# Small tiles regrouped and padded so that every large SBUF tile begins on a multiple of 128 bytes

## The chip, the cores and the metric

The kernel runs on one core of a Trainium2 chip. Its time is the device time of one launch in microseconds (us); the number compared is the median over several runs. The engines are named as in the profile: PE (TensorE, matmuls; PEld is its weight load), DVE (VectorE), ACT (ScalarE), POOL (GpSimd) and SP (SyncE, which here only issues DMAs). SBUF is the on-chip memory of 128 partitions; an address in this text is a byte offset within a partition, the same in every partition.

## The reference

A two-layer decoder trunk over 512 tokens of width 1024, in float32. Each layer computes

```
x = x + 1/2 * swiglu(rmsnorm(x), ffn1)          # 1024 -> 2816 -> 1024
h = rmsnorm(x); p = h @ w_in                    # 1024 -> 6168 columns
x = x + concat(mlstm(p), ssd(p), convmodule(p)) @ w_out
x = x + 1/2 * swiglu(rmsnorm(x), ffn2)
```

and after both layers a last rmsnorm. `swiglu(h) = (silu(h @ wg) * (h @ wu)) @ wd`. mlstm and ssd are recurrences done in chunks of 128 tokens, the conv module is a depthwise convolution of width 31.

## The kernel before, in words

**Data and precision.** The residual x lies in SBUF transposed, as eight tiles xT[k] of 128 features by 512 tokens. A float32 product is made of three matmuls in a reduced type of 4 bytes: each operand is split into a high and a low part (xh/xl, whi/wlo, atile pairs, chi/clo), and high*high, high*low and low*high are accumulated in PSUM. Almost all of PE's work is such matmuls with a stationary operand of 128x128 (loaded by PEld) and a moving operand of 128x512 (2048 bytes in each partition).

**The families of matmuls.** They differ in which tile is stationary and which is moving:

- L189 to L191 (mm3) has a weight slice stationary (whi or wlo) and 512 tokens moving. In `contraction` the moving tile is an atile (the activations of a block), in `proj` it is xh or xl.
- L354 to L356 (product_halves in `gated`) has activations stationary and 512 weight columns moving (whi or wlo). The activations are slices of xh/xl, or of chi/clo, which hold sums and differences of x for a Strassen-like scheme: of the seven products of a block three take xh/xl and four take chi/clo.
- L877 to L879 (tok_proj, in the mixer) has xh/xl stationary and whi/wlo moving.
- L1059 to L1061 (Final.finish, the last contraction) has an atile stationary and whi/wlo moving: the form of L354 to L356 and L877 to L879, with other tiles.

```
189  nc.tensor.matmul(ps, wh, ah, start=start and k == 0, stop=False)     # out, stationary, moving
190  nc.tensor.matmul(ps, wh, al, start=False, stop=False)
191  nc.tensor.matmul(ps, wl, ah, start=False, stop=stop and k == n - 1)
354  nc.tensor.matmul(ps[t], ah, hv[:, i, :], start=start and k == 0, stop=False, **more)
355  nc.tensor.matmul(ps[t], ah, lv[:, i, :], start=False, stop=False, **more)
356  nc.tensor.matmul(ps[t], al, hv[:, i, :], start=False, stop=k == 3, **more)
877  nc.tensor.matmul(pv[c], xh[k][:, cs(c)], hv[:, k2, :], start=k == 0, stop=False)
1059 nc.tensor.matmul(ps, ah, hv[:, k - k0, :], start=k == 0, stop=False)
```

Every slice of these operands begins a multiple of 512 bytes past the start of its tile. Smaller matmuls in float32 proper (transposes such as L418, the scores and state products of the mixer such as L728, L807 and L839) make up the rest.

**The order of the work.** Each of the four FFNs is one first block of 256 hidden columns and five gated blocks of 512. A gated block is 168 matmuls of L354 to L356, 16 transposes (L418) and 96 matmuls of a contraction (L189 to L191). Between the two FFNs of a layer lies the mixer: projections (L189 to L191 with xh/xl moving, L877 to L879), the chunked recurrences, the 31-tap convolution as 30 DVE instructions per tile (L690), and contractions into xT. Weights stream from HBM into raw or half (SP queue), ACT casts them to whi (L175) and DVE makes wlo (L176), three buffers each. A scheduler orders the instructions by priority; addresses have no part in it.

**Where tiles lie.** A pool places its tiles one after the other in the order in which their tags are first asked for; each start is rounded up to 32 bytes, and a pool begins where the one before ends. The pools stand in the order const, wp, ap, tp, and then the phase's own pool (ff0, mix0, ff1, ...). const begins on a multiple of 128. Before the change:

| pool | tiles in order | start of the large tiles, modulo 128 |
|---|---|---|
| const (L93 to L108) | ident, ones, tri (512 bytes each), eps_r, eps_l (4 each, 32 taken), xT, xh, xl (24 of 2048), two upads, parameter columns | xT, xh, xl, upad: 64 |
| wp | raw (3 of 8192), whi and wlo (3 of 4096 each) | 0 |
| ap | 12 atiles of 2048 | 0 |
| tp | pst 512, ssq0 64 (L1125), ss, tmp (2048 each), rc 4 of 32, R 2048, nr 2 and den 4 of 32, fss 32 (L1052) | ss, tmp, R: 64 |
| FFN phases | half and chi/clo (4096 each), u (2048) | all: 32 |
| mixer phases | brow 224, dt to ecs 256 each, av, en, ws, dec, gw, arow, lt, rt, cacc, mtile, mc, rb, sc, small, wide, xb | cacc, mtile: 32; rb, sc, wide, first xb: 96 |

Of the kernel before, what the change touches and what calls it, by code (L numbers as in the profile page):

```python
# [20 lines left out]
F32 = mybir.dt.float32  # L21
# [6 lines left out]
P = 128  # L28
# [3 lines left out]
NCH = S // P  # L32
MH = 4
# [3 lines left out]
RMS_EPS = 1e-6  # L37
LN_EPS = 1e-5
# [11 lines left out]
def trunk(ctx: ExitStack, tc: tile.TileContext, I: dict, out: bass.AP):  # L50
    nc = tc.nc
# [4 lines left out]
    const = ctx.enter_context(tc.tile_pool(name="const", bufs=1))  # L56
    wp = ctx.enter_context(tc.tile_pool(name="wp", bufs=1))
    ap_ = ctx.enter_context(tc.tile_pool(name="ap", bufs=1))
    tp = ctx.enter_context(tc.tile_pool(name="tp", bufs=1))
# [12 lines left out]
    mp_ = Phase()  # L72
# [4 lines left out]
    def pacc():  # L77
        return ps_p.tile([P, S], F32, tag="acc", name="pacc")
# [4 lines left out]
    def tmp():  # L83
        return tp.tile([P, S], F32, tag="t", name="tmp", bufs=6)
# [4 lines left out]
    def mtile():  # L89
        return mp_.tile([P, S], F32, tag="m", name="mtile", bufs=9)  # L90


    ident = const.tile([P, P], F32, name="ident")  # L93
    make_identity(nc, ident)
    ones = const.tile([P, P], F32, name="ones")
# [1 line left out]
    tri = const.tile([P, P], F32, name="tri")  # L97
    nc.gpsimd.affine_select(tri, ones, pattern=[[1, P]], base=0, channel_multiplier=-1,
                            compare_op=ALU.is_ge, fill=0.0)
    eps_r = const.tile([P, 1], F32, name="eps_r")  # L100
    nc.vector.memset(eps_r, RMS_EPS)
    eps_l = const.tile([P, 1], F32, name="eps_l")
    nc.vector.memset(eps_l, LN_EPS)

    xT = [const.tile([P, S], F32, name=f"xT{k}") for k in range(KT)]
    xh = [const.tile([P, S], F32R, name=f"xh{k}") for k in range(KT)]
# [1 line left out]
    upads = [const.tile([P, S + CK - 1], F32, name=f"upad{i}") for i in range(2)]  # L108
    for t in upads:
        nc.gpsimd.memset(t[:, 0:CK - 1], 0.0)  # L110

    @contextmanager
    def shifted(n):
# [30 lines left out]
    def stream(src, nk, n):  # L144
        with shifted(-early[0]):
            raw = wp.tile([P, 2048], F32, tag="raw", name="raw", bufs=3)
            v = raw[:, :nk * n].rearrange("p (k n) -> p k n", n=n)
            k0 = c0 = 0
            for s in src if isinstance(src, list) else [src]:
                k, w = s.shape[1:]  # L150
                nc.sync.dma_start(v[:, k0:k0 + k, c0:c0 + w], s)
                k0, c0 = (k0, c0 + w) if k == nk else (k0 + k, c0)
        return v
# [14 lines left out]
    def split_w(v):  # L168
        with shifted(-early[0]):
            nk, n = v.shape[1], v.shape[2]  # L170
            hi = wp.tile([P, 1024], F32R, tag="whi", name="whi", bufs=3)
            lo = wp.tile([P, 1024], F32R, tag="wlo", name="wlo", bufs=3)
            hv = hi[:, :nk * n].rearrange("p (k n) -> p k n", n=n)
            lv = lo[:, :nk * n].rearrange("p (k n) -> p k n", n=n)
            nc.scalar.copy(hv, v)  # L175
            nc.vector.tensor_tensor(lv, v, hv.bitcast(F32), op=sub)  # L176
        return hv, lv
# [44 lines left out]
    class Norm:  # L222
# [24 lines left out]
        def finish(self):  # L247
            self.R = tp.tile([P, S], F32, tag="R", name="R", bufs=1)
            with shifted(AFTER):
                self.r = tp.tile([P, NCH], F32, tag="nr", name="nr", bufs=2)  # L250
                stat(self.ss, D, eps_r, self.r) if self.sums is None else rstd_cols(self.sums, D, eps_r, self.r)
                nc.scalar.copy(self.R, rows(self.r))
            return self
# [237 lines left out]
    def mixer(l, nrm, par, nxt):  # L491
# [4 lines left out]
        def cols(c0, n):  # L496
            return W[:, :, c0:c0 + n]
# [3 lines left out]
        nc.gpsimd.dma_start(graw[:, :, 0:8], cols(C_I, 8))  # L501
        nc.gpsimd.dma_start(graw[:, :, 8:24], cols(C_DT, 16))
        brow = mp_.tile([P, 56], F32, tag="brow", name="brow")
        nc.gpsimd.dma_start(brow[:, 0:8], I["mlstm_gate_b"][l:l + 1, :].partition_broadcast(P))
        nc.gpsimd.dma_start(brow[:, 8:24], I["ssd_dt_bias"][l:l + 1, :].partition_broadcast(P))
        nc.gpsimd.dma_start(brow[:, 24:40], I["ssd_a_log"][l:l + 1, :].partition_broadcast(P))
# [2 lines left out]
        sm = lambda n, nm: mp_.tile([P, n], F32, tag=nm, name=nm)  # L509
# [6 lines left out]
        av = sm(16, "av").rearrange("p (c h) -> p c h", h=MH)  # L516
        en = sm(16, "en").rearrange("p (c h) -> p c h", h=MH)
        ws = sm(12, "ws").rearrange("p (c h) -> p c h", h=MH)
        dec = sm(8, "dec")
        ml_rows = dr.tile([MH, 7 * P], F32, tag="ml_rows", name="ml_rows", bufs=1)  # L520
        ml_dec = dr.tile([1, MH * 2], F32, tag="ml_dec", name="ml_dec", bufs=1)
        cs = lambda c: slice(c * P, (c + 1) * P)
# [2 lines left out]
        def gates():  # L525
# [15 lines left out]
            part = lambda o, n: scratch[:, o:o + n]  # L541
# [8 lines left out]
            s1 = part(176, 80).rearrange("p (c h) -> p c h", h=20)  # L550
            s2 = part(256, 80).rearrange("p (c h) -> p c h", h=20)
            lp = part(336, 80).rearrange("p (c h) -> p c h", h=20)
            arow = sm(16, "arow")
            with tc.issue_after(nc.scalar.activation(e, gt[:, :, 4:24], AF.Abs).ins):
                nc.scalar.activation(arow, brow[:, 24:40], AF.Exp)
            nc.scalar.activation(e, e, AF.Exp, scale=-1.0)
# [47 lines left out]
                nc.tensor.transpose(pl[0:MH, c * P:(c + 1) * P], lc[:, c, 0:4], ident)  # L604
            nc.vector.tensor_copy(ar, pa[0:MH, :])
            nc.vector.tensor_copy(lr, pl[0:MH, :])
            mc = sm(16, "mc")[0:MH, :]
            for c in range(NCH):
                init = NEG if c == 0 else mc[:, c - 1:c]
                nc.vector.tensor_tensor_scan(Mx[:, cs(c)], ar[:, cs(c)], ar[:, cs(c)], init, op0=mx, op1=mx)  # L610
# [418 lines left out]
    class Final:  # L1029
# [19 lines left out]

        def finish(self, acts, wrows, scale):  # L1050
            nk = len(acts)
            ss = tp.tile([P, 2 * NCH], F32, tag="fss", name="fss")  # L1052
            ov = out.rearrange("b (c p) d -> p (b c) d", p=P)

            def mms(ps, c, k0, sp):
                hv, lv = sp
                for k in range(k0, k0 + 2):
                    ah, al = [t[:, c * P:(c + 1) * P] for t in acts[k]]
                    nc.tensor.matmul(ps, ah, hv[:, k - k0, :], start=k == 0, stop=False)  # L1059
                    nc.tensor.matmul(ps, ah, lv[:, k - k0, :], start=False, stop=False)  # L1060
                    nc.tensor.matmul(ps, al, hv[:, k - k0, :], start=False, stop=k == nk - 1)  # L1061

            def done(ps, c, q):
                o = self.o[q][c]
                nc.vector.scalar_tensor_tensor(o, ps, scale, o, op0=mul, op1=add)
                nc.scalar.activation(tmp(), o, AF.Square, accum_out=ss[:, q * NCH + c:q * NCH + c + 1])
                self.o[q][c] = t = tmp() if q else o
                nc.vector.tensor_tensor(t, o, self.g[q], op=mul)

            def w(q):  # L1070
                v = stream(wrows[:, q * S:(q + 1) * S].rearrange("(k p) d -> p k d", p=P), nk, S)
                for k in range(0, nk, 2):
                    yield k, split_w(v[:, k:k + 2, :])

            acc = [pacc(), pacc(), pacc(), pmix()]
            for k, sp in w(0):
                for c in range(NCH):
                    mms(acc[c], c, k, sp)
            sps = list(w(1))
            for c in range(NCH):  # L1080
                done(acc[c], c, 0)
            for c in range(NCH):
                ps = pacc()
                for k, sp in sps:
                    mms(ps, c, k, sp)
                done(ps, c, 1)
                r = tp.tile([P, 2], F32, tag="den", name="fr", bufs=4)[:, 0:1]
                nc.vector.tensor_tensor(r, ss[:, c:c + 1], ss[:, NCH + c:NCH + c + 1], op=add)
                nc.scalar.activation(r, r, AF.Sqrt, bias=eps_r, scale=1.0 / D)
                nc.vector.reciprocal(r, r)  # L1090
                nc.scalar.mul(self.o[0][c], self.o[0][c], r)
                nc.vector.tensor_scalar(self.o[1][c], self.o[1][c], r, None, op0=mul)
                for q in range(2):
                    [nc.scalar, nc.sync][q].dma_start(ov[:, c, q * S:(q + 1) * S], self.o[q][c])
# [27 lines left out]
    load_w(1, 1)  # L1122
    with tc.manual_schedule(engines={mybir.EngineType.PE, mybir.EngineType.DVE, mybir.EngineType.Activation}):
        px, sp = {}, []
        ssq = tp.tile([P, NCH, 4], F32, tag="ssq0", name="ssq0")  # L1125

        def take(q):
            for k in (2 * q, 2 * q + 1):
# [127 lines left out]
```

## Time and profile before

| what | value |
|---|---|
| median of 3 runs | 2285.18 us (2284.99 to 2288.55) |
| the profiled execution | 2285.9 us |
| its span, first to last instruction | 2284.2 us |
| granted TensorE clock, mean of the span | 0.997 |

The profile is of one execution. The span is what its timeline covers; 1.7 us of the execution's time lie around it. Windows and timelines below are in us from the start of the span. A matmul's printed duration contains its passage through the array, which overlaps the next matmul; how often PE starts one is read from the start times of two rows and the number of matmuls between them.

### The profile page before, as it was taken

The page shows a single profiled execution, that of the slowest core. Times are in us where ns is not written, and L with a number is a line of the kernel's source. Part 1 is how long each engine was busy: PE and PEld are TensorE (multiplying, and loading weights), DVE is VectorE, ACT ScalarE, POOL GpSimd, SP SyncE. Part 2 cuts the span into 40 slices and gives each one's busy share as a digit, 9 for nine tenths or more (in the row PEclk, how much of TensorE's full clock was granted, in tenths as well). Part 3 has the DMA queues.
Part 4 walks back from the last instruction along what each step waited for, and adds up shares of the span by engine and source line. Part 5 has one row for each costly group of instructions (what it writes and reads, how often), then busy time and mean ns, then how long its engine had stood idle before and what let it go on. Part 6 is the DMA issues. An engine that isn't in the chain of part 4 may idle for free.

```text
span 2284.2 us, 26881 instructions
## 1 busy us (share of the span) xinstructions
PE 2250.6 (99%) x10339; PEld 1836.7 (80%) x10339; DVE 1824.0 (80%) x2517; ACT 1126.3 (49%) x1633; POOL 83.0 (4%) x145
## 2 busy tenths in 40 slices
PE   8899999999999999999999999999999999999998
PEld 6688888788888878888878888877888888788887
DVE  7877787999966787777797777688999588877776
ACT  5433345767555543334443344366665555433334
POOL 0000000100110000000000000001101000000000
PEclk9999999999999999999999999999999999999999
DMA  5333313333332242332233332133323324332221
GB/s 185 112 101 103 107 42 95 112 93 93 111 99 72 83 140 83 111 111 92 74 111 111 111 111 93 56 95 93 111 81 110 95 67 149 105 106 90 91 83 47
DMA packets 146016, 224.70 MB, mean 98 GB/s; under 512 B 6584, under 2 KB 66392, under 8 KB 145888
## 3 DMA queue, kind: packets, MB, share of 16 engines
q1 hardware_dynamic: 139712, 208.68, 28.9%
q0 software_dynamic: 5088, 13.14, 2.1%
q8 instruction: 82, 1.34, 0.2%
q10 hardware_dynamic: 1088, 1.16, 0.1%
q14 instruction: 46, 0.38, 0.1%
HBM read 220.77 MB, written 2.19 MB: 98 GB/s over the span
## 4 chain that ended last, share of the span: by engine, by line
PE 92%; DVE 3%; ACT 2%; issue 1%; DMA 1%; POOL 0%; SPq 0%; POOLq 0%; ACTq 0%
PE pacc L189 14%; PE pacc L190 14%; PE pacc L191 14%; PE pacc L355 10%; PE pacc L354 10%; PE pacc L356 10%; PE pacc L877 3%; PE pacc L878 2%; PE pacc L879 2%; PE pmix L355 2%; PE pmix L354 2%; PE pmix L356 2%; PE pmix L418 1%; PE pmix L839 1%; DVE wlo L176 1%
## 5 line engine op out<-in xcount | busy, mean ns | idle before, releaser
L175 ACT CAST whi<-raw 128x1024 fp32r<-128x1024 f32 (+1 forms) x276 | 285.8, 1036 | 411.5 <-PE pacc L190 214.1
L175 ACT CAST whi<-half 128x1024 fp32r<-128x1024 f32 x240 | 251.2, 1047 | 404.5 <-PE pacc L356 202.4
L176 DVE TENSOR_TENSOR wlo<-raw,whi 128x1024 fp32r<-128x1024 f32 (+1 forms) x276 | 332.5, 1206 | 119.2 <-ACT whi L175 112.8
L176 DVE TENSOR_TENSOR wlo<-half,whi 128x1024 fp32r<-128x1024 f32 x240 | 293.4, 1223 | 135.1 <-ACT whi L175 135.1
L189 PE MATMUL pacc<-atile,whi 128*128 128x512 f32 x928 | 364.2, 394 | 4.6 <-DVE xT L327 4.2
L190 PE MATMUL pacc<-atile,whi 128*128 128x512 f32 x928 | 362.3, 390 | 0.3
L191 PE MATMUL pacc<-atile,wlo 128*128 128x512 f32 x928 | 362.3, 390 | 0.0
L189 PE MATMUL pacc<-xh,whi 128*128 128x512 f32 x608 | 243.8, 401 | 0.0
L191 PE MATMUL pacc<-xh,wlo 128*128 128x512 f32 x608 | 239.4, 394 | 0.0
L190 PE MATMUL pacc<-xl,whi 128*128 128x512 f32 x608 | 238.8, 393 | 0.0
L189 PEld LDWEIGHTS pacc<-atile,whi 128*128 128x128 f32 x928 | 174.0, 188 | 50.1 <-DVE xT L327 14.7
L327 DVE SCALAR_TENSOR_TENSOR xT<-pacc,xT 128x512 f32<-128x512 f32 x184 | 126.2, 687 | 102.1 <-PE pacc L191 100.7
L190 PEld LDWEIGHTS pacc<-atile,whi 128*128 128x128 f32 x928 | 174.3, 188 | 37.0 <-DVE atile L182 1.6
L191 PEld LDWEIGHTS pacc<-atile,wlo 128*128 128x128 f32 x928 | 174.3, 188 | 36.4
L354 PE MATMUL pacc<-whi,chi 128*128 128x512 f32 x480 | 189.3, 396 | 7.0 <-ACT whi L175 7.0
L355 PE MATMUL pacc<-wlo,chi 128*128 128x512 f32 x480 | 192.3, 401 | 0.0
L354 PE MATMUL pacc<-whi,xh 128*128 128x512 f32 x480 | 191.0, 398 | 0.0
L356 PE MATMUL pacc<-whi,xl 128*128 128x512 f32 x480 | 189.8, 395 | 0.0
L355 PE MATMUL pacc<-wlo,xh 128*128 128x512 f32 x480 | 189.8, 395 | 0.0
L356 PE MATMUL pacc<-whi,clo 128*128 128x512 f32 x480 | 188.6, 393 | 0.0
L690 DVE SCALAR_TENSOR_TENSOR cacc<-upad,pA,cacc 128x512 f32<-128x512 f32 x240 | 176.5, 767 | 1.1
L361 DVE TENSOR_TENSOR half<-half 128x1024 f32<-128x1024 f32 x120 | 145.7, 1217 | 0.9
(330 smaller groups left out, 3720.1 us busy)
## 6 DMA issues: line engine op xcount, KB each, us to landing
raw<-in_ffn_w_down_dram SPq DMA_DIRECT2D x44, 1024.0 KB, 5.0
half<-in_ffn_w_up_dram SPq DMA_DIRECT2D x80, 512.0 KB, 3.7
raw<-in_w_in_dram SPq DMA_DIRECT2D x40, 1024.0 KB, 5.4
raw<-in_ffn_w_gate_dram SPq DMA_DIRECT2D x23, 1024.0 KB, 5.1
half<-in_ffn_w_gate_dram SPq DMA_DIRECT2D x40, 512.0 KB, 4.6
raw<-in_w_out_dram SPq DMA_DIRECT2D x10, 1024.0 KB, 5.0
raw<-in_w_in_dram SPq DMA_DIRECT2D x16, 512.0 KB, 4.6
rb<-ssd_rows POOLq DMA_DIRECT2D x32, 256.0 KB, 4.1
```

Of the source, the lines that this page charges most:

```text
L175: nc.scalar.copy(hv, v)
L176: nc.vector.tensor_tensor(lv, v, hv.bitcast(F32), op=sub)
L189: nc.tensor.matmul(ps, wh, ah, start=start and k == 0, stop=False)
L190: nc.tensor.matmul(ps, wh, al, start=False, stop=False)
L191: nc.tensor.matmul(ps, wl, ah, start=False, stop=stop and k == n - 1)
L327: nc.vector.scalar_tensor_tensor(xT[d], ps, scale, xT[d], op0=mul, op1=add)
L354: nc.tensor.matmul(ps[t], ah, hv[:, i, :], start=start and k == 0, stop=False, **more)
L355: nc.tensor.matmul(ps[t], ah, lv[:, i, :], start=False, stop=False, **more)
L356: nc.tensor.matmul(ps[t], al, hv[:, i, :], start=False, stop=k == 3, **more)
L361: nc.vector.tensor_tensor(v, v, w, op=add)
L690: nc.vector.scalar_tensor_tensor(o, u[:, j:j + S], col(cA, j * 4 + c), o, op0=mul, op1=add)
L877: nc.tensor.matmul(pv[c], xh[k][:, cs(c)], hv[:, k2, :], start=k == 0, stop=False)
```

## The change

Only the places of tiles in SBUF change; every instruction stays and keeps its order. In const, eps_r and eps_l go behind the upads. In tp, ssq0 grows from 64 to 128 bytes (its users take the first four of eight columns) and fss from 32 to 64. In the mixer's pool, dec and mc are asked for earlier and arow becomes a part of an existing scratch tile. The tile sizes then add up so that xT, xh, xl, upad, ss, tmp, R, half, chi/clo, u, gw, cacc, mtile, rb, sc, wide and the first xb begin on a multiple of 128. wp and ap stay where they were. The second xb and three of the four small tiles (1548 bytes, 1568 taken) keep odd starts.

```diff
@@ const
-    eps_r = const.tile([P, 1], F32, name="eps_r")
-    nc.vector.memset(eps_r, RMS_EPS)
-    eps_l = const.tile([P, 1], F32, name="eps_l")
-    nc.vector.memset(eps_l, LN_EPS)
 
     xT = [const.tile([P, S], F32, name=f"xT{k}") for k in range(KT)]
...
     for t in upads:
         nc.gpsimd.memset(t[:, 0:CK - 1], 0.0)
+    eps_r = const.tile([P, 1], F32, name="eps_r")
+    nc.vector.memset(eps_r, RMS_EPS)
+    eps_l = const.tile([P, 1], F32, name="eps_l")
+    nc.vector.memset(eps_l, LN_EPS)
@@ mixer
         brow = mp_.tile([P, 56], F32, tag="brow", name="brow")
+        dec = mp_.tile([P, 8], F32, tag="dec", name="dec")
...
         ws = sm(12, "ws").rearrange("p (c h) -> p c h", h=MH)
-        dec = sm(8, "dec")
+        mc = sm(16, "mc")[0:MH, :]
...
-            arow = sm(16, "arow")
+            arow = part(496, 16)
...
-            mc = sm(16, "mc")[0:MH, :]
@@ Final.finish
-            ss = tp.tile([P, 2 * NCH], F32, tag="fss", name="fss")
+            ss = tp.tile([P, 4 * NCH], F32, tag="fss", name="fss")
@@ first loads
-        ssq = tp.tile([P, NCH, 4], F32, tag="ssq0", name="ssq0")
+        ssq = tp.tile([P, NCH, 8], F32, tag="ssq0", name="ssq0")[:, :, 0:4]
```

## Rows read from the trace of the kernel before

**Rows 1.** The page's part 1: busy us (share) xinstructions of each engine, whole span.

```profile
PE 2250.6 (99%) x10339; PEld 1836.7 (80%) x10339; DVE 1824.0 (80%) x2517; ACT 1126.3 (49%) x1633; POOL 83.0 (4%) x145
```

**Rows 2.** The page's part 4: the chain that ended last, share by engine.

```profile
PE 92%; DVE 3%; ACT 2%; issue 1%; DMA 1%; POOL 0%; SPq 0%; POOLq 0%; ACTq 0%
```

**Rows 3.** Window of one gated block: its bounds, us, busy by engine, granted clock, DMA.

```profile
1225.42:1288.46 63.04, 63.04 (x283) 51.20 (x281) 47.46 (x53) 24.42 (x28) 0.00 (x0) 1.00 0.32 101
```

**Rows 4.** Waits of PE, whole span, the two costliest: us in total, times, longest.

```profile
PE pacc L354 <- ACT whi L175: 7.0, 1, 7.0
PE pmix L626 <- ACT atile L622: 4.6, 2, 3.2
```

**Rows 5.** Timeline of PE, contraction, first row and the 91st (start us, us, ...).

```profile
1478.08 0.39 PE L189 MATMUL pacc<-atile,whi 128*128 128x512 f32 x1
...
1498.48 0.40 PE L189 MATMUL pacc<-xh,whi 128*128 128x512 f32 x1
```

**Rows 6.** Timeline of PE, last contraction: first row and the 64th.

```profile
2256.86 0.39 PE L1059 MATMUL pacc<-whi,atile 128*128 128x512 f32 x1
...
2271.15 0.39 PE L1059 MATMUL pacc<-whi,atile 128*128 128x512 f32 x1
```

**Rows 7.** Timeline of PE, gated block with chi/clo: first row and the 73rd.

```profile
1441.29 0.39 PE L354 MATMUL pmix<-whi,chi 128*128 128x512 f32 x1
...
1458.09 0.39 PE L354 MATMUL pacc<-whi,xh 128*128 128x512 f32 x1
```

**Rows 8.** Timeline of PE, gated block with xh/xl: first row and the 37th.

```profile
1405.95 0.39 PE L354 MATMUL pacc<-whi,xh 128*128 128x512 f32 x1
...
1414.35 0.71 PE L418 MATMUL pmix<-ident,tmp 128*128 128x128 f32 x5
```

**Rows 9.** Timeline of PE, mixer's tok_proj: first row and the 155th.

```profile
654.86 0.39 PE L877 MATMUL pacc<-whi,xh 128*128 128x512 f32 x1
...
690.79 0.49 PE L751 MATMUL pmix<-ident,mtile 128*128 128x128 f32 x3
```

**Rows 10.** Timeline of PE, proj with xh/xl moving: first row and the 74th.

```profile
1515.39 0.40 PE L190 MATMUL pacc<-xl,whi 128*128 128x512 f32 x1
...
1532.12 0.43 PE L190 MATMUL pacc<-xl,whi 128*128 128x512 f32 x1
```

**Rows 11.** Groups by line and form, whole span: counts of the families (one line of three).

```profile
L189 PE MATMUL pacc<-xh,whi 128*128 128x512 f32 x608 | 243.8, 401 | 0.0
...
L354 PE MATMUL pacc<-whi,xh 128*128 128x512 f32 x480 | 191.0, 398 | 0.0
...
L354 PE MATMUL pacc<-whi,chi 128*128 128x512 f32 x480 | 189.3, 396 | 7.0 <-ACT whi L175 7.0
...
L877 PE MATMUL pacc<-whi,xh 128*128 128x512 f32 x256 | 102.2, 401 | 0.3 <-DVE mtile L643 0.3
...
L354 PE MATMUL pmix<-whi,chi 128*128 128x512 f32 x160 | 63.0, 394 | 0.0
```

**Rows 12.** The first mixer: its window (columns as Rows 3).

```profile
410.00:750.00 340.00, 337.14 (x1662) 279.77 (x1661) 291.84 (x491) 215.00 (x374) 29.95 (x48) 1.00 0.31 96
```

**Rows 13.** The chain that ended last, pieces of the first mixer and one gated block: start, us, what.

```profile
560.03 0.89 PE pmix L728 x8
561.25 0.87 PE pmix L807 x8
...
644.61 1.05 DVE cacc L690
...
1288.46 1.75 PE pmix L418 x16
```

**Rows 14.** Groups by line and form, DVE: same residue and mixed residues.

```profile
L176 DVE TENSOR_TENSOR wlo<-raw,whi 128x1024 fp32r<-128x1024 f32 x260 | 317.2, 1222 | 119.2 <-ACT whi L175 112.8 <-PE pmix L947 5.0 <-PE pmix L820 0.6
L176 DVE TENSOR_TENSOR wlo<-half,whi 128x1024 fp32r<-128x1024 f32 x240 | 293.4, 1223 | 135.1 <-ACT whi L175 135.1
...
L361 DVE TENSOR_TENSOR half<-half 128x1024 f32<-128x1024 f32 x120 | 145.7, 1217 | 0.9
...
L361 DVE TENSOR_TENSOR half<-half,raw 128x1024 f32<-128x1024 f32 x40 | 49.0, 1226 | 1.4
```

## The prediction

> **What bounds the kernel now.** I read the page's busy shares first, then the chain, then the window of one block, and last the start times of single matmuls.
>
> PE is busy 99% of the span, DVE 80%, ACT 49% [rows 1]. Busy time alone proves little for PE, since a printed matmul overlaps the next one, so the chain decides: 92% of the work that ended last is on PE [rows 2]. A gated block shows it from nearer: it takes 63.0 us, with PE busy throughout and DVE for 47.4 us, at a granted clock of 1.00, which is the upper level, 2.4 GHz [rows 3]. PE's costliest wait of the whole span is 7.0 us, once, for the first gated block's weights, and the next is 4.6 us in two pieces [rows 4]. So the time is the number of matmuls times the spacing at which PE starts them, and what matters is whether that spacing depends on addresses.
>
> It seems to. All big matmuls are of one form, 128x128 stationary and 128x512 moving, yet they start at three spacings:
>
> - Contraction, atile moving and whi/wlo stationary, both on multiples of 128: 90 matmuls in 20.40 us, 226.7 ns each [rows 5].
> - Gated blocks, stationary chi/clo at 32 past a multiple: 72 in 16.80 us, 233.3 ns [rows 7]. Stationary xh/xl at 64 past: 36 in 8.40 us, again 233.3 ns [rows 8]. The mixer's tok_proj, stationary xh/xl: 154 in 35.93 us, 233.3 ns [rows 9].
> - proj, xh/xl moving at 64 past, stationary whi/wlo on a multiple: 73 in 16.73 us, 229.2 ns [rows 10].
>
> The families differ in more than address: in the second, activations are stationary and weights move. The control is the last contraction, which has just that form (activations stationary, whi/wlo moving, the same order high-high, high-low, low-high), but its activations are atiles, on multiples of 128: 63 matmuls in 14.29 us, 226.8 ns [rows 6]. Exchanging the operands thus costs nothing; what is left to tell 226.7 from 233.3 is where the stationary tile begins. I take it that a stationary operand off a multiple of 128 costs 6.6 ns and a moving one 2.5 ns (229.2 less 226.7). That 32 and 64 past cost the same says that the step is not at 32 or 64 bytes.
>
> **The change, part by part.** No instruction, DMA or wait is added or removed, and no queue's order changes. After it the operands of all these families begin on a multiple of 128. By the layout in front they even share the residue of the fast families in larger powers: whi, atile, xh and chi all then begin 128 bytes past a multiple of 512.
>
> 1. *Gated blocks.* Three lines of 480 + 480 + 160 matmuls [rows 11] are 3360; times 6.6 ns is 22.2 us, 1.1 us in each of the 20 blocks. A block now is 168 x 233.3 ns + 96 x 226.7 ns + 1.75 us for 16 transposes [rows 13] = 62.7 us of its 63.0 us, so PE has 0.3 us of slack in it; DVE has 15.6 us [rows 3]. Nothing else is near, and a block should come to 61.9 us. I count 95%, 21.1 us: where an FFN begins a block can wait for casts, as the first one does [rows 4].
> 2. *tok_proj.* 3 x 256 = 768 [rows 11] x 6.6 ns = 5.1 us.
> 3. *proj.* 3 x 608 = 1824 [rows 11] x 2.5 ns = 4.6 us.
> Terms 2 and 3 lie nearly all in the two mixers, where PE is busy 337 of 340 us but DVE 292 and ACT 215 [rows 12], and where stretches of the chain run through DVE, not PE, as in the convolution near 645 us [rows 13]. There a faster PE arrives earlier and waits. I count 75% of 9.7 us, 7.3 us, between none and all.
> 4. *Small float32 matmuls.* Groups of eight take 0.89 us where both operands lie off (L728) and 0.87 us where only one does (L807) [rows 13]; no row shows these shapes with both on a multiple. Per matmul that is some 2.5 ns; about 1400 of them give 3.4 us at most, nothing at least, since many of their operands (the second xb, small) stay off. I take 1 us.
> 5. *DVE and ACT.* A DVE pass over 128x1024 takes 1222 ns with all operands on 128 and 1223 ns with one of them at 32 past [rows 14], so these engines gain nothing, and need not, being off the path.
> 6. *The edits themselves.* eps_r and eps_l are still set on DVE before their first use; the strided ssq0 feeds one reduction behind the first products; arow goes into a scratch tile that the instruction ahead of it on ACT has to have anyway. Mixer tiles lie over FFN tiles of the phase before and wait for their release; the shift is of some 100 bytes in tiles of 4096, so nearly all partners stay, and mc, which moves far, lies over chi/clo tiles that are done before the gates are computed. Cost nothing; if a load came later, PE still has projections to do, and the bound is a microsecond or two per mixer.
>
> Sum: 21.1 + 7.3 + 1 = 29.4 us. Against the profiled execution, 2285.9 us (a span of 2284.2 us and 1.7 us around it), that gives 2256.5 us. The median of the runs, 2285.18 us, is 0.7 us below that execution, so I say 2256 us.
>
> **The rivals.**
>
> *No change.* The spacing would belong to the tiles' use and not to their addresses, for example to the traffic of other engines around each family, and the time stays 2285 us. For it: no family shows one tile at two residues. Against it: the control [rows 6], and that each of the slow spacings is the same to 0.1 ns in tiles of two pools and two phases [rows 7 to 9]. The Trainium skill, in "SBUF — State Buffer", Specifications (TRN2), gives SBUF lines of 16 bytes, and "TensorE: Matmul & The Clock Gate", Back-to-back issue gap, gives a spacing by columns and clock alone, some 216 ns for 512 columns at the upper clock. By these pages every start before the change is already on a line, and the time stays 2285 us; the three spacings in the trace disagree with a rule of columns alone. Chance 5%.
>
> *The gain is taken up elsewhere.* The spacing falls, but PE then waits for casts or DVE in the mixers and at block ends, so that terms 2 to 4 vanish and half of term 1 is kept: 11 us, 2274 us. For it: DVE pieces in the chain [rows 13]. Against it: 15.6 us of DVE slack per block [rows 3], and no group of waits of PE on DVE or ACT over 7.0 us in the whole run [rows 4]. Chance 4%.
>
> *Slower.* With every large tile on the same residue, the two inputs and the output of a DVE instruction always meet on it; if that made DVE's passes slower, the mixers, where DVE has 14% of slack (292 of 340 us), would become DVE's. To eat the 21 us that the FFNs keep, DVE's 292 us in each mixer would have to exceed its 340 us by 10.5 us, that is grow by 20%; at 25% each mixer would end near 365 us, 25 us later, and with 21 us kept in the FFNs the time would be some 2314 us. Against it: halves added to halves, all at one residue, take 1217 ns, and with raw, at another, 1226 ns [rows 14]; sharing a residue is no slower. Chance 2%.
>
> **How the numbers follow.** The forecast, with all its parts, has 89%. Its fast end is all of terms 1 to 3 and the upper bound of 4: 22.2 + 5.1 + 4.6 + 3.4 = 35.3 us, 2250 us. Its slow end keeps 80% of term 1 and nothing of the others: 17.8 us, 2267 us. That range leaves out the rivals, 11%, and little more. A difference of 0.2%, 4.6 us, is about what a measurement of this kernel can tell from none. Faster by more than that: the forecast and the second rival, 93%. Within it: 5%. Slower: 2%.
>
> **What would show it.** In the profile after, the same runs of matmuls should stand at 226.7 ns in all families; a gated block should repeat every 61.9 us; DVE's passes should keep their lengths; PE's waits in the mixers should grow by 2 to 3 us. If chi/clo falls to 226.7 ns and xh/xl does not, or the other way round, the cause is in the tile and not in its start. If all spacings fall and the time does not, the second rival is right. If the spacings stay at 233.3 ns, the premise is wrong.

## The result, and the profile after

| | before | after |
|---|---|---|
| median, 4 runs each | 2286.86 us (2284.99 to 2289.85) | 2261.86 us (2259.18 to 2263.24) |
| ratio of the two | | 0.9888, 95% interval 0.9871 to 0.9905 |
| the profiled execution, its span | 2285.9, 2284.2 us | 2261.44, 2259.6 us |

The change saves 25.0 us, 1.1%, inside the range and 5.9 us short of the forecast of 2256. Lines behind the first edit stand one line later in the changed kernel (L355 is L354 of before).

The busy shares and the chain of the changed kernel (the page's parts 1 and 4):

```profile
PE 2223.3 (98%) x10339; PEld 1836.8 (81%) x10339; DVE 1821.9 (81%) x2517; ACT 1126.1 (50%) x1633; POOL 82.8 (4%) x145
...
PE 86%; DVE 8%; ACT 3%; issue 2%; DMA 1%; POOL 1%; SPq 0%; ACTq 0%; POOLq 0%; DVEq 0%
```

PE is busy 27.3 us less with the same 10339 instructions; DVE and ACT have moved by 2.1 us at most [rows 1]. Of the chain, PE has lost six points of 92%, mostly to DVE and ACT [rows 2].

Where the 27 us are is read as before, from the start times of the same matmuls. The timeline of PE in the changed kernel, for each family the first row and the one behind its last: contraction, gated chi/clo, gated xh/xl, tok_proj, proj:

```profile
1461.56 0.39 PE L190 MATMUL pacc<-atile,whi 128*128 128x512 f32 x1
...
1481.98 0.39 PE L190 MATMUL pacc<-xh,whi 128*128 128x512 f32 x1
...
1425.42 0.39 PE L355 MATMUL pmix<-whi,chi 128*128 128x512 f32 x1
...
1441.74 0.39 PE L355 MATMUL pacc<-whi,xh 128*128 128x512 f32 x1
...
1390.63 0.39 PE L355 MATMUL pacc<-whi,xh 128*128 128x512 f32 x1
...
1398.79 0.82 PE L419 MATMUL pmix<-ident,tmp 128*128 128x128 f32 x6
...
650.04 0.40 PE L878 MATMUL pacc<-whi,xh 128*128 128x512 f32 x1
...
684.99 0.49 PE L752 MATMUL pmix<-ident,mtile 128*128 128x128 f32 x3
...
1498.73 0.39 PE L191 MATMUL pacc<-xl,whi 128*128 128x512 f32 x1
...
1515.40 0.45 PE L191 MATMUL pacc<-xl,whi 128*128 128x512 f32 x1
```

| family | matmuls | before, ns | after, ns |
|---|---|---|---|
| contraction [rows 5] | 90 | 226.7 | 20.42 us / 90 = 226.9 |
| gated chi/clo [rows 7] | 72 | 233.3 | 16.32 / 72 = 226.7 |
| gated xh/xl [rows 8] | 36 | 233.3 | 8.16 / 36 = 226.7 |
| tok_proj [rows 9] | 154 | 233.3 | 34.95 / 154 = 226.9 |
| proj [rows 10] | 73 | 229.2 | 16.67 / 73 = 228.4 |

Four families stand at one spacing. proj came only part of the way in this stretch; over all its matmuls the mean time from one start to the next, gaps over 260 ns left out, went from 229.3 to 227.3 ns.

Two windows of the changed kernel, the first mixer and one gated block, from the chain's transposes at 929.16 us to those at 991.15 us:

```profile
395.00:735.00 340.00, 335.85 (x1661) 281.00 (x1660) 293.67 (x494) 214.45 (x363) 30.07 (x48) 0.99 0.32 97
929.16:991.15 61.99, 61.99 (x284) 51.24 (x282) 47.34 (x53) 24.60 (x29) 2.49 (x5) 1.00 0.33 103
```

A block is 1.05 us shorter, with PE still busy throughout and DVE's 47 us unchanged [rows 3]. The mixer is not such a stage: in its 340 us PE works 1.3 us less than before and DVE 1.8 us more, and its granted clock has fallen from 1.00 to 0.99 [rows 12].

Comparing the start times of the same matmuls at the bounds of the stages, the FFNs took 19.6 us less (the first 4.0, the two in the middle 10.6 together, the last 5.0) and the two mixers 3.9 (1.0 and 2.9). Another 1.0 us lies ahead of the first matmul, whose wait for a load (L134, now L135) was 3.4 us and is 2.4 us. That one varies with the execution and not with the layout: the first matmul starts at 3.40 us in the profile before and at 3.46 in that of e5, below, and at 2.34 to 2.82 us in the other ten profiles, the old layout with an edit elsewhere (e9) among them. 19.6 + 3.9 + 1.0 is the 24.5 us of the span.

### The profile page after: what moved, and what is told of

Read it like the earlier page. It is cut to its first block, busy times and chain, and to the rows that moved or that the text cites. A ratio compares the mean times of both kernels' runs of the same rounds, so it can differ in the third digit from the quotient of the medians.

```text
span 2259.6 us, 26881 instructions
## 1 busy us (share of the span) xinstructions
PE 2223.3 (98%) x10339; PEld 1836.8 (81%) x10339; DVE 1821.9 (81%) x2517; ACT 1126.1 (50%) x1633; POOL 82.8 (4%) x145
## 3 DMA queue, kind: packets, MB, share of 16 engines
q8 instruction: 82, 1.34, 0.2%
## 4 chain that ended last, share of the span: by engine, by line
PE 86%; DVE 8%; ACT 3%; issue 2%; DMA 1%; POOL 1%; SPq 0%; ACTq 0%; POOLq 0%; DVEq 0%
PE pacc L190 13%; PE pacc L191 13%; PE pacc L192 13%; PE pacc L356 9%; PE pacc L355 9%; PE pacc L357 9%; PE pacc L878 2%; PE pacc L880 2%; PE pacc L879 2%; DVE wlo L177 2%; PE pmix L356 2%; PE pmix L357 2%; PE pmix L355 2%; ACT whi L176 1%; DVE half L362 1%
## 5 line engine op out<-in xcount | busy, mean ns | idle before, releaser
L355 PE MATMUL pacc<-whi,chi 128*128 128x512 f32 x480 | 186.9, 391 | 7.0 <-ACT whi L176 7.0
L355 PE MATMUL pacc<-whi,xh 128*128 128x512 f32 x480 | 188.2, 392 | 0.0
L356 PE MATMUL pacc<-wlo,chi 128*128 128x512 f32 x480 | 187.6, 391 | 0.0
```

## The experiments

The theory of the prediction was that a large tile's start should be a multiple of 128. The main rival grew out of a remark there, that whi, atile, xh and chi would also *share* a residue: then what counts is the distance between the starts of the two operands. Diffs are against the changed kernel unless they say otherwise. "Difference" below is the moving tile's start less the stationary tile's.

### The change again, and its two parts

e1 is the changed kernel once more.

> The changed kernel once more, beside fresh runs of the kernel before, to narrow the interval and to see which parts of its trace recur. Theory (a start off a multiple of 128 costs a stationary operand 6.6 ns and a moving one 2.5 ns): a ratio of 0.988 to 0.990, a gated block at 62.0 us, mean spacing of the big matmuls 227.1 ns. If the fall of the granted clock near 427 us in the first mixer was chance, it is missing here and the span is 1 to 2 us shorter; if it follows from the longer wait of the gate transposes, it is there again.

It took 2261.52 us (2260.89 to 2262.38), ratio 0.9886 [0.9871, 0.9901].

e2 keeps only the move of eps in const: xT, xh, xl aligned, chi/clo still at 32.

```diff
-        dec = mp_.tile([P, 8], F32, tag="dec", name="dec")
-        mc = sm(16, "mc")[0:MH, :]
-            arow = part(496, 16)
-            ss = tp.tile([P, 4 * NCH], F32, tag="fss", name="fss")
-        ssq = tp.tile([P, NCH, 8], F32, tag="ssq0", name="ssq0")[:, :, 0:4]
+        dec = sm(8, "dec")
+            arow = sm(16, "arow")
+            mc = sm(16, "mc")[0:MH, :]
+            ss = tp.tile([P, 2 * NCH], F32, tag="fss", name="fss")
+        ssq = tp.tile([P, NCH, 4], F32, tag="ssq0", name="ssq0")
```

> Only eps_r and eps_l moved behind the upads: xT, xh, xl, upad on multiples of 128, everything from tp on as before (half, chi/clo at 32). Theory: gated matmuls with xh/xl stationary and tok_proj fall to 227 ns, proj to 227 ns, those with chi/clo stay at 233.3 ns; a gated block falls by 72 x 6.3 ns = 0.45 us to 62.6 us; the whole by 1440 x 6.3 ns = 9 us in the FFNs and some 4 us in the mixers, to about 0.994. Rival (the tile's use sets the spacing, or one shift moves all families together): either all families move here or none.

e3 is the other part alone: the pools' edits, with eps back in front of xT.

```diff
+    eps_r = const.tile([P, 1], F32, name="eps_r")
+    nc.vector.memset(eps_r, RMS_EPS)
+    eps_l = const.tile([P, 1], F32, name="eps_l")
+    nc.vector.memset(eps_l, LN_EPS)
 
     xT = [const.tile([P, S], F32, name=f"xT{k}") for k in range(KT)]
...
-    eps_r = const.tile([P, 1], F32, name="eps_r")
-    nc.vector.memset(eps_r, RMS_EPS)
-    eps_l = const.tile([P, 1], F32, name="eps_l")
-    nc.vector.memset(eps_l, LN_EPS)
```

> The other part alone: eps_r and eps_l in front as before (xT, xh, xl at 64), tp and the phase pools padded as in the change (half, chi/clo, u, mixer tiles on multiples of 128). Theory: only chi/clo falls, from 233.3 to 227 ns; xh/xl stationary stays at 233.3 ns and moving at 229.2 ns; a gated block falls by 96 x 6.3 ns = 0.6 us to 62.4 us; the whole by 1920 x 6.3 ns = 12 us, at 90% on the path some 11 us, to about 0.995; the two parts together make the whole change. Rival as in the other part.

e2: 2275.63 us, ratio 0.995 [0.9937, 0.9962]. e3: 2276.85 us, ratio 0.9953 [0.994, 0.9965]. Against the 2287.50 us of the kernel before, measured beside them, that is 11.9 and 10.7 us, as much as was expected of each; together 22.5 of the 26.0 us that e1 gains there. The timeline of PE shows that each part frees its own tiles. e2, gated chi/clo:

```profile
1435.51 0.39 PE L354 MATMUL pmix<-whi,chi 128*128 128x512 f32 x1
...
1452.31 0.40 PE L354 MATMUL pacc<-whi,xh 128*128 128x512 f32 x1
```

The same 72 matmuls in e3:

```profile
1433.73 0.39 PE L355 MATMUL pmix<-whi,chi 128*128 128x512 f32 x1
...
1450.08 0.40 PE L355 MATMUL pacc<-whi,xh 128*128 128x512 f32 x1
```

In e2 chi/clo stays at 16.80 us / 72 = 233.3 ns while tok_proj falls to 226.9; in e3 chi/clo is at 16.35 / 72 = 227.1 and tok_proj stays at 233.3. So a family's spacing follows the place of its own tile. That rules out a cause in the families' use of their tiles, the first rival of the prediction, but both theories of the address still stand.

### Everything at 32 past a multiple of 128

One eps tile stands in front of xT and the second upad grows by 64 bytes, so that raw, whi, wlo, atile, xh, xl, chi and clo all begin 32 past a multiple of 128.

```diff
+    eps = const.tile([P, 2], F32, name="eps")
+    eps_r, eps_l = eps[:, 0:1], eps[:, 1:2]
...
     xT = [const.tile([P, S], F32, name=f"xT{k}") for k in range(KT)]
...
-    upads = [const.tile([P, S + CK - 1], F32, name=f"upad{i}") for i in range(2)]
+    upads = [const.tile([P, S + CK - 1 + 16 * i], F32, name=f"upad{i}")[:, 0:S + CK - 1] for i in range(2)]
```

> As the changed kernel, but every large tile, raw, whi, wlo and the atiles too, begins 32 bytes past a multiple of 128: all share one residue, and none is on a multiple. Theory (the absolute start counts): every big matmul has both operands off, its spacing is 233.3 ns at least and 235.8 ns if the two prices add, also in the contraction, which the change left alone; 8900 matmuls by 6.2 to 8.7 ns are 55 to 78 us more than the changed kernel, a ratio to the kernel before of 1.012 to 1.023. Rival (what counts is that stationary and moving operand share a residue, as they do in every fast family so far): all stay at 227 ns, ratio 0.989. Second rival (the collision of equal residues slows DVE): the same DVE durations as in the changed kernel either way, since residues are equal in both.

2261.17 us, ratio 0.9888 [0.9874, 0.9901]: the whole gain. Its timeline of PE, gated chi/clo, then xh/xl:

```profile
1423.69 0.39 PE L355 MATMUL pmix<-whi,chi 128*128 128x512 f32 x1
...
1440.01 0.39 PE L355 MATMUL pacc<-whi,xh 128*128 128x512 f32 x1
...
1388.92 0.39 PE L355 MATMUL pacc<-whi,xh 128*128 128x512 f32 x1
...
1397.08 0.82 PE L419 MATMUL pmix<-ident,tmp 128*128 128x128 f32 x6
```

16.32 us / 72 = 226.7 ns and 8.16 / 36 = 226.7 ns, with no operand on a multiple of 128 or of 64. The theory of absolute starts has fallen; equal residues stand.

### Unequal distances, and the step

e7 keeps xh, xl, chi and clo on multiples of 128 and puts the weights and atiles 64 past one: the distance of before between proj's operands, but now in the gated blocks, and the other way round.

```diff
-    upads = [const.tile([P, S + CK - 1], F32, name=f"upad{i}") for i in range(2)]
+    upads = [const.tile([P, S + CK - 1 + 16 * i], F32, name=f"upad{i}")[:, 0:S + CK - 1] for i in range(2)]
...
-        ssq = tp.tile([P, NCH, 8], F32, tag="ssq0", name="ssq0")[:, :, 0:4]
+        ssq = tp.tile([P, NCH, 4], F32, tag="ssq0", name="ssq0")
```

> The changed kernel with raw, whi, wlo and the atiles at 64 modulo 128 and all else on multiples: the residues of the kernel before with the parts exchanged. Theory (difference of residues, dearer when the two stand in the order stationary off, moving on or the other way about does not matter): contraction, both at 64, 227 ns; gated blocks and tok_proj (stationary 0, moving 64) and proj (stationary 64, moving 0) slow again. If the price hangs on the role that is off a multiple, gated and tok_proj stand at 229 ns and proj at 233 ns, exchanged against before, 4128 x 2.3 + 1824 x 6.3 ns = 21 us over the changed kernel at most, about 2277 us. If it hangs on the family, gated and tok_proj stand at 233 ns and proj at 229 ns: 4128 x 6.3 + 1824 x 2.3 = 30 us at most, about 2287 us.

2278.28 us, ratio 0.9954 [0.9939, 0.9969]. The timeline of PE, gated chi/clo, then proj:

```profile
1436.50 0.39 PE L355 MATMUL pmix<-whi,chi 128*128 128x512 f32 x1
...
1452.98 0.39 PE L355 MATMUL pacc<-whi,xh 128*128 128x512 f32 x1
...
1510.28 0.40 PE L191 MATMUL pacc<-xl,whi 128*128 128x512 f32 x1
...
1527.31 0.39 PE L191 MATMUL pacc<-xl,whi 128*128 128x512 f32 x1
```

16.48 us / 72 = 228.9 ns, and 17.03 / 73 = 233.3 ns: the prices of before have changed places, and the time is the 2277 us or so that was expected for that. These two spacings by themselves would still fit the premise, since the operand off a multiple of 128 is now the moving one in the gated blocks and the stationary one in proj. The contraction does not fit it: both its operands are now 64 past a multiple of 128, and it keeps 226.8 ns. Together with e4 this says that a difference of the two starts has the price, and that its sign counts: with the moving tile 64 ahead some 229 ns (proj before, gated blocks here), with it 64 behind 233.3 (gated xh/xl before, proj here).

e5 gives the xh tiles four residues, so that one program holds several differences.

```diff
-    xh = [const.tile([P, S], F32R, name=f"xh{k}") for k in range(KT)]
+    xh = []
+    for k in range(KT):
+        xh.append(const.tile([P, S], F32R, name=f"xh{k}"))
+        if k == 1:
+            eps_r = const.tile([P, 1], F32, name="eps_r")
...
+        if k == 3:
+            eps_l = const.tile([P, 1], F32, name="eps_l")
...
+        if k == 5:
+            g1col = const.tile([P, KT], F32, tag="g1", name="g1", bufs=1)
```

> The changed kernel with xh0,1 at 0, xh2,3 at 32, xh4,5 at 64, xh6,7 at 96 and all of xl at 96 modulo 128; whi, wlo, atile, chi/clo stay at 0. Theory now (after all tiles at 32 ran as fast as all at 0): what costs is a stationary and a moving operand of different residues modulo 128. It expects 227 ns at xh0,1 with neighbours of their own kind, 233 ns where xh2..7 or xl are stationary and 229 ns where they move, whichever of 32, 64, 96 it is. Rival: the price grows with the distance or is tied to 64, so that 32, 64 and 96 give three different spacings.

One execution took 2275.4 us; tok_proj stood at 232.3 ns, proj at 232.3, chi/clo, which kept its place, at 226.8. Neither 233 and 229 ns by the operand's role nor a price that grows with the distance came out; the table below has the distances one by one.

e5b puts the upads between xh tiles: xh2 and xh3 begin 128 from the weights' residue modulo 256, the last four and xl 256 from it modulo 512, and the rest share it.

```diff
-    xh = [const.tile([P, S], F32R, name=f"xh{k}") for k in range(KT)]
+    xh, upads = [], []
+    for k in range(KT):
+        xh.append(const.tile([P, S], F32R, name=f"xh{k}"))
+        if k in (1, 3):
+            upads.append(const.tile([P, S + CK - 1], F32, name=f"upad{k // 2}"))
...
-    upads = [const.tile([P, S + CK - 1], F32, name=f"upad{i}") for i in range(2)]
```

> The changed kernel with the two upads (2176 bytes each) put between the xh tiles: xh0,1 begin at 128, xh2,3 at 256, xh4 to 7 and xl at 384 modulo 512; all are multiples of 128 and whi/wlo stay at 128 modulo 512. Theory (only the difference modulo 128 counts): all spacings stay at 227 ns and the time at the changed kernel's. Rival (the step is 256 or 512): where xh2 to xh7 or xl is stationary 233 ns, where it moves 229 ns, and a gated block of 62.5 us.

One execution took 2266.43 us, 4.6 us over the changed kernel's median. Tiles 256 away from their partner were as fast as at 0 (gated xh/xl, 36 matmuls at 226.8 ns, 24 of them at a distance of 256 and 12 at 0), tiles 128 away were slow. A step of 128 was what I had expected until here, so this theory fell too: the step is 256.

With the starts known from the layout, every big matmul can be sorted by its difference modulo 256. The mean time from its start to the next start, gaps over 260 ns left out, groups of over 200:

| moving less stationary, modulo 256 | matmuls and ns, by kernel |
|---|---|
| 0 | before 2793 at 227.5; after 8696 at 227.1; e4 8699 at 227.1; e5b 8124 at 227.5; e5 some 4700 (contractions, chi/clo) at 227.1, and some 540 (xh0, xh1) at 231.5 |
| 32 | e5 323 at 231.4 |
| 64 | before (proj) 1834 at 229.3; e7 (gated, tok_proj) 4079 at 229.1; e5 316 at 230.4 |
| 96 | before (chi/clo) 1920 at 233.3; e5 940 at 233.5 |
| 128 | e5b 586 at 231.7; e8, below, 5932 at 232.5 |
| 160 | e5 1180 at 231.8 |
| 192 | before (gated xh/xl, tok_proj) 2163 at 233.2; e7 (proj) 1850 at 233.3; e5 446 at 233.6 |
| 224 | e5 274 at 232.6 |

One row is fast, where whole families are in it. The others cost 2 to 6 ns with no plain order by distance; in e5 and e5b neighbours of different rows follow each other, so their means are less clean than the others'.

These mixed kernels also show that a matmul's own two operands do not settle its time. In e5 the matmuls with xh0 and xh1 are at a difference of 0, but of every three matmuls in such a stretch one is with xl, at another difference. Those with xh0 and xh1 take 231.5 ns, not the 227 that was expected of them among their own kind. In e5b's gated blocks and tok_proj, matmuls at 0 followed by another at 0 take 226.8 ns (3632 of them) and those followed by one at 128 take 232.7 (124). The timelines of PEld and PE in e5b, where tok_proj comes to xh2:

```profile
671.59 0.19 PEld L881 LDWEIGHTS pacc<-whi,xh 128*128 128x128 f32 x1
...
671.58 0.40 PE L883 MATMUL pacc<-whi,xl 128*128 128x512 f32 x1
671.82 0.40 PE L881 MATMUL pacc<-whi,xh 128*128 128x512 f32 x1
672.06 0.40 PE L882 MATMUL pacc<-wlo,xh 128*128 128x512 f32 x1
```

L883's own operands are 256 apart, and yet the next matmul starts 233 ns behind it (unrounded); while it runs, the slice of xh2 for that next matmul is being loaded. The next two take 240 ns each. So the rule that the runs support is one for runs of matmuls: a stretch is fast when all operands that meet or follow each other in it share the residue modulo 256.

### All on multiples of 128, and unequal modulo 256

The sharpest test: every large tile keeps a multiple of 128, but weights and atiles move on by 128, to 0 modulo 256, while xh, xl, chi and clo stay at 128.

```diff
-        ssq = tp.tile([P, NCH, 8], F32, tag="ssq0", name="ssq0")[:, :, 0:4]
+        ssq = const.tile([P, NCH, 8], F32, tag="ssq0", name="ssq0")[:, :, 0:4]
```

> The changed kernel with raw, whi, wlo and the atiles moved up by 128 bytes (ssq0's 128 bytes now lie in front of them): every large tile still begins on a multiple of 128, but weights and atiles on a multiple of 256 and xh, xl, chi/clo 128 past one. Theory now (what counts is that stationary and moving operand share their residue modulo 256): gated blocks, tok_proj and proj are slow again although everything is on a multiple of 128, the time is some 15 to 25 us over the changed kernel, ratio 0.994 to 0.999. Rival (the start on a multiple of 128 is what counts, and the slow spacings of xh2 and xh3 in the run with the upads between had another cause): 227 ns everywhere, ratio 0.989.

2288.09 us (11 runs) against 2288.69 us (21 runs of before), ratio 0.9995 [0.9986, 1.0004]: what the change is described as doing gains nothing by itself. The ratio is just above the 0.994 to 0.999 that was expected, since proj too went up, to 232.6 ns over all its matmuls from 229.3 before. The timeline of PE in this kernel, contraction, chi/clo and tok_proj, and the window of one gated block:

```profile
1476.74 0.40 PE L190 MATMUL pacc<-atile,whi 128*128 128x512 f32 x1
...
1497.15 0.40 PE L190 MATMUL pacc<-xh,whi 128*128 128x512 f32 x1
...
1440.04 0.40 PE L355 MATMUL pmix<-whi,chi 128*128 128x512 f32 x1
...
1456.78 0.40 PE L355 MATMUL pacc<-whi,xh 128*128 128x512 f32 x1
...
654.22 0.40 PE L878 MATMUL pacc<-whi,xh 128*128 128x512 f32 x1
...
690.01 0.49 PE L752 MATMUL pmix<-ident,mtile 128*128 128x128 f32 x3
```

```profile
1224.71:1287.58 62.87, 62.86 (x283) 51.29 (x281) 47.42 (x53) 24.41 (x28) 0.00 (x0) 1.00 0.32 101
```

The contraction, whose operands moved together, keeps 20.41 us / 90 = 226.8 ns; chi/clo is back at 16.74 / 72 = 232.5 and tok_proj at 35.79 / 154 = 232.4. The block is at 62.87 us, near the 63.04 of before.

### The gate transposes of the mixer, later

This asks where the mixers' gain stayed. PE's waits in the changed kernel:

```profile
PE pacc L355 <- ACT whi L176: 7.0, 1, 7.0
PE pmix L627 <- ACT atile L623: 5.4, 2, 3.2
PE pacc L190 <- DVE xT L328: 4.8, 7, 1.1
```

The wait at L627 has grown from 4.6 to 5.4 us [rows 4]. In the first mixer its neighbourhood reads so, in the windows ahead of the wait's end, behind it, and then:

```profile
423.00:425.67 2.67, 0.47 (x4) 0.05 (x2) 1.89 (x5) 2.66 (x9) 0.00 (x0) 1.00 0.00 0
425.67:426.90 1.23, 1.23 (x5) 0.74 (x5) 1.23 (x3) 1.23 (x3) 0.00 (x0) 1.00 0.00 0
426.90:430.20 3.30, 3.30 (x8) 2.00 (x8) 2.57 (x4) 2.79 (x6) 0.00 (x0) 0.50 0.88 268
430.20:433.00 2.80, 2.80 (x16) 2.37 (x16) 2.32 (x6) 0.63 (x1) 0.00 (x0) 0.98 0.18 64
```

PE stands still for some 2.2 us, works for 1.2 us at the upper level, and then has a granted clock of 0.50, 1.2 GHz, for 3.3 us, in which it starts 8 matmuls where the next 2.8 us hold 16. Before, the same transposes wait 1.4 us and the clock stays at 1.00. The fall comes again in e1, at 427 us, so it is no chance of one execution. The second mixer has one such fall in either kernel. But the longer wait does not come again. The first of these transposes and the windows behind it, before, then in e1:

```profile
430.19 0.22 PE L626 MATMUL pmix<-ident,atile 4*128 4x4 f32 x1 [1.40 <-ACT atile L622]
430.20:434.00 3.80, 3.80 (x17) 2.53 (x18) 3.80 (x7) 3.41 (x7) 0.00 (x0) 1.00 0.55 155
...
425.47 0.22 PE L627 MATMUL pmix<-ident,atile 4*128 4x4 f32 x1 [1.34 <-ACT atile L623]
427.30:430.70 3.40, 3.40 (x11) 2.32 (x11) 2.45 (x5) 2.19 (x5) 0.00 (x0) 0.50 0.91 303
```

With a wait of 1.34 us the clock falls in e1, with 1.40 it stays up before: the length of this wait alone does not decide.

e6 lets these transposes stand some 24 matmuls later in PE's order; the layout is the changed one.

```diff
-            pe = pmix()
-            for c in range(3):
-                nc.tensor.transpose(pe[:, c * MH:(c + 1) * MH], ar[:, cs(c)], ident[0:MH, 0:MH])
+            with shifted(90):
+                pe = pmix()
+                for c in range(3):
+                    nc.tensor.transpose(pe[:, c * MH:(c + 1) * MH], ar[:, cs(c)], ident[0:MH, 0:MH])
...
```

> The changed kernel with the last transposes of the gates (seven small matmuls and their two copies) put some 20 matmuls later in PE's order in both mixers, by a lower priority. Theory (part of the mixers' gain is lost where PE arrives earlier at these transposes, waits for ACT, and the granted clock falls after the wait): the waits of 5.4 us go, the clock's falls near 427 us and 1540 us go, and the time falls by 4 to 8 us against the changed kernel, to a ratio of about 0.985 to 0.987. Rival (the wait is for the ACT chain and just moves to the next thing that needs it): the same ratio as the changed kernel, 0.9886.

2257.68 us (2256.09 to 2258.13), ratio 0.9863 [0.9847, 0.988]: faster than both kernels. The group is gone from PE's waits:

```profile
PE pacc L355 <- ACT whi L176: 7.0, 1, 7.0
PE pacc L190 <- DVE xT L328: 4.8, 7, 1.1
PE pacc L1133 <- DMA raw<-in_x_dram: 3.0, 1, 3.0
```

and a window over the place in this kernel shows the clock at 1.00:

```profile
426.00:436.00 10.00, 9.56 (x41) 6.71 (x40) 9.84 (x17) 8.01 (x15) 0.00 (x0) 1.00 0.34 107
```

The mixers are 2.4 and 2.7 us shorter than in the changed kernel. Whether that is gain that the layout had left lying, or worth as much on any layout, e9 asks: the same edit on the kernel before.

> The kernel before, with its old layout, and the last gate transposes put later as in the run before. If the wait at these transposes ate part of what the change gained in the mixers, the same edit is worth less here than on the changed kernel: the kernel before waits 4.6 us there and the clock falls once, near 1556 us, so 2 to 3 us, a ratio of 0.9988 to 0.9991. Rival (the edit is worth as much with either layout, and the wait is no part of the difference): 4 to 5 us, ratio 0.998.

2284.01 us (11 runs), ratio 0.9981 [0.9973, 0.999]: 4.7 us, more than the 2 to 3 that were expected and about what the edit gives on the changed layout, as the rival has it. With the edit in both kernels the layout is worth 0.9863 / 0.9981 = 0.988, no more than without it. In the single profiles the first mixer gains 0.85 us by it on the old layout and 2.4 on the new one, which fits one fall of the clock more; in the second, where either kernel has a fall, it gains 2.5 and 2.7. The medians don't resolve the difference.

## Why the prediction was right, and on a wrong premise

**The bound.** Right. PE set the time, the spacing of its matmuls depends on where tiles lie, and the spacing after was read off the fast families correctly: 226.7 predicted, 226.7 to 226.9 measured in four of five.

**The premise.** Wrong. "A stationary operand off a multiple of 128 costs 6.6 ns, a moving one 2.5 ns" explains the rows of before, but e4, with everything 32 off, is as fast as the change, and e8, with everything on 128, is as slow as before. What the runs showed is the table above: a run of matmuls is fast when its operands begin at equal residues modulo 256. The control [rows 6] had shown only that exchanging the operands is free; its tiles were aligned *and* shared a residue, so it could not tell the two apart. The numbers came out because the change also gives whi, atile, xh and chi/clo the same residue, 128, which the prediction noted and did not use. In that the number was luck. The role of an operand was the sign of a difference: 128 less 192 before, for xh stationary, and 192 less 128 for xh moving.

**Term 1, the gated blocks.** 21.1 us predicted, 19.6 measured in the FFNs: blocks at 62.0 us, not 61.9, and the first FFN gave 4.0 of its 5.2 (five blocks by 1.05), since the time from the first matmul to the first block's transposes did not shorten (99.36 us before, 99.52 after, and 97.8 to 102.0 in the other ten profiles): there PE waits for loads and casts [rows 4].

**Terms 2 to 4, the mixers.** The step that was mis-sized: 7.3 + 1 us predicted, 3.9 measured, so 40% of the 9.7 was kept and not 75%. The spacings did fall: tok_proj by 6.4 ns, and proj by 0.8 in the stretch shown but from 229.3 to 227.3 as a mean over all its matmuls, 2.0 of the predicted 2.5. 768 x 6.4 and 1824 x 2.0 ns are 8.6 us; 0.7 us of it lies in the FFNs, where a fifth of the proj matmuls stand, and half of the rest was given back. The starts of the same matmuls in both traces, taken pair by pair from the first proj of a mixer to its last contraction, tell where. The big matmuls gave 7.4 us in the two mixers. In the first, 1.4 us went back where the clock was at 0.50, 1.3 on longer waits of PE (0.8 of it at the gate transposes) and 0.2 on the rest; in the second, 0.6 on waits and 0.4 on the rest. By these bounds 3.5 us are left. So the waits grew by 1.9 us, a little under the predicted 2 to 3, and the fall of the clock, for which the prediction has no term, comes on top. In e1 the first mixer gives back 1.5 us to the clock again but only 0.2 to waits, so of the two only the fall recurs. These are single profiles: since the edit of e9 was worth as much on the old layout, the medians do not bear out either. Term 4 can't be told from nothing: the eight small matmuls of L728 start 112 ns apart before and after.

**Terms 5 and 6, DVE, ACT and the edits.** Right. Groups by line and form of the changed kernel, DVE:

```profile
L177 DVE TENSOR_TENSOR wlo<-raw,whi 128x1024 fp32r<-128x1024 f32 x260 | 317.4, 1223 | 111.9 <-ACT whi L176 108.6
...
L362 DVE TENSOR_TENSOR half<-half 128x1024 f32<-128x1024 f32 x120 | 145.7, 1218 | 0.9
L362 DVE TENSOR_TENSOR half<-half,raw 128x1024 f32<-128x1024 f32 x40 | 49.0, 1225 | 1.4
```

They are within 1 ns of [rows 14], with all inputs and outputs at one residue; the mechanism of the slower rival is not there: where their tiles begin made no difference to these passes.

**The rivals.** "No change" fell with e2 and e3. The Trainium skill's "TensorE: Matmul & The Clock Gate", Back-to-back issue gap, has a formula for the gap of a single matmul, by columns and clock alone; the stream of matmuls in the trace does not follow it, with 227 to 233 ns for one shape at one granted clock. The Trainium skill's "SBUF — State Buffer", Specifications (TRN2), gives lines of 16 bytes. They do not separate the cases either: every start here is on such a line. "The gain is taken up elsewhere" held for more than half of the mixers' part and for nothing of the blocks.

**Left open.** Why equal residues are fast is not shown. That PE reads the next weights (PEld) while it streams the moving tile, and that the two reads meet where starts differ, would be a story to these numbers. The trace shows the overlap, and e5b's rise one matmul ahead of xh2 is in its favour. Against it as it stands, the last matmul before xh4 in that stretch, with its own operands 256 apart and the next ones too, still takes 231 ns. No run took the reads apart. Distances that are no multiple of 32, other shapes and other types were not tried. Every slice began a multiple of 512 bytes past its tile, so the rule is told for tiles' starts alone.

## What to carry to other kernels

Where PE is the bound, compare the start times of matmuls of one shape by which tiles they read; spacings that differ by a few per cent, each constant within a tile, point at the layout. Give all tiles that meet in a matmul the same start modulo 256, pools of weights and of activations alike; rounding each to 128 by itself gains nothing (0.9995 in e8). The neighbours count too, so it is whole stretches that have to agree. And before one believes a rule of addresses from the rows, one should name the row that would tell "aligned" from "alike".

## What I had not expected of the hardware

- The spacing of a 128x512 matmul depends on the difference of its operands' starts modulo 256: 226.8 ns at 0 (and at 256), 229 to 234 ns at seven other multiples of 32. No absolute alignment that was tried mattered. A matmul at 0 is slow too when the one behind it is not (232.7 ns in e5b).
- The price depends on the sign: 229.1 to 229.3 ns with the moving tile 64 ahead, 233.2 to 233.3 ns with it 64 behind.
- The granted clock fell to 0.50 for 3.4 us some 1.2 to 1.8 us after PE had waited at the gate transposes, 2.2 us in the changed kernel and 1.34 in its repeat, and did not fall at that place after the 1.40 us of before; each time it cost some 1.4 us, and no row tells what decided.
